# Full 128-row, 128-column weights for the products of a triangular inversion, and a new order of the front's pieces, in a two-layer encoder on one core

## The chip, the core and the metric

The kernel runs on one core of one Trainium2 chip. The metric is device microseconds of one launch, the median of several launches. The engines named here are TensorE (PE, with PEld for its loads of weights), VectorE (DVE), ScalarE (ACT), GpSimd (POOL) and SyncE (SP), which issues the DMAs.

## What is computed

Two encoder layers over 512 tokens of width 1024. Each layer has a differential attention branch, a gated delta rule in both directions (four heads, chunks of 64 tokens), gates that merge the two, and an MLP. The change touches the triangular solve in the delta rule, and the order of the work ahead of it:

```python
L = jnp.where(strict, jnp.einsum('bhncd,bhnmd->bhncm', kb, k) * decay, 0.0)
T = lax.linalg.triangular_solve(eye + L, jnp.broadcast_to(eye, L.shape), left_side=True,
                                lower=True, unit_diagonal=True)
u = jnp.einsum('bhncm,bhnme->bhnce', T, v * beta[..., None])
```

## The kernel before, in words

The kernel treats the 512 tokens as four tiles (NT) of 128. It first records every operation with its operands. A planner (`Plan.schedule`) then lists the recorded operations onto five in-order queues (PE, ACT, DVE, POOL, SP). It uses the costs of the function `cost`, priorities, and the free buffers of each pool. What a queue holds is fixed when the program is built, and at run time each engine waits at its own head. So a plan that puts an instruction too early makes that engine wait, with everything behind it. All operations carry one line of the kernel file, L431, where they are issued, so tiles are told apart by name.

In each layer a "front" comes after the first norm. It is a list of pieces in the string `ORDER[l]`: `d` (three projections of one delta-rule head, with a convolution on DVE), `z` (its gate's projection), `q`, `k`, `v` (projections for two attention heads), `a` (chunk matrices of a delta-rule head), `b` (inversion of the 32x32 diagonal blocks of two heads, a chain of small DVE operations on the tile XA), `c` (the rest of a head's delta rule) and `t` (one attention head). The recording order is only the planner's priority. The engines' real order follows from the plan.

Names that the steps need: `d_dn`, `d_z`, `d_da` and `d_g` are PSUM tiles of the dense projections. Their products take weights and activations in a split form (`whi`, `wlo` and `hh`, `hl`), and `wlo_...` is made on DVE. `kqv` is a projection after its convolution (`cacc`) and activation. `tokT` is its transpose on PE. `qkT`, `rot` and `dt` belong to attention's q and k. `zg` is the gate of `z`.

The products of the inversion stand in `gdn_c`, once for each layer, head and direction d. `pn` multiplies L by the inverse of its diagonal blocks, giving `NTr`. Then three products `px` (n = 1, 2, 3) extend X by one band of 32 columns (NB) each. Each of these is a group of four matmuls in float32, one for each token tile; the trace holds two records for each float32 matmul. With two layers, four heads, two directions and four products there are 64 groups. The call `four(name, lhsT, rhs, rows, cs)` has `lhsT` as weights and `rhs` as the moving operand. In the kernel before, the weights are only the rows that are needed:

```python
rows, cs = (slice(0, m), slice(NB * n, P)) if d == 0 else (slice(0 if n == 1 else P - m, P), slice(0, m))
ps, op = four("px", NTr[ks, :, rows], X[ks, d, :, cs], rows, cs)
```

with m = 96, 64, 32. So the weights are 96 (d = 0) or 128 (d = 1) columns wide for n = 1, 64 for n = 2 and 32 for n = 3, and the moving operand has 96, 64 and 32 columns. For `pn` the weights have 128 columns (d = 0) or 96 (d = 1), and the moving operand 96.

Of the kernel before, what the change touches and what calls it, by code (L numbers as in the profile page):

```python
# [17 lines left out]
P = 128  # L18
# [12 lines left out]
NB = 32  # L31
# [153 lines left out]
class Plan:  # L185
# [13 lines left out]
    def add(self, engs, fn, args, kw):  # L199
# [37 lines left out]
        op.shared = fn != "memset" and not any(v.t.cls == "B" for v in ins + outs)  # L237
        op.tried = set()
        op.cost = [cost(e, fn, dst, ins, kw) for e in engs]
        self.ops.append(op)  # L240
        return op
# [209 lines left out]
def cost(eng, fn, dst, ins, kw):  # L451
    n = int(np.prod(dst.shape[1:]))
    ptr = sum(isinstance(kw.get(k), View) for k in ("scalar", "scalar1", "scale", "bias"))
    psum = any(v.t.cls == "B" for v in ins)
    if ins:
        n = max([n] + [int(np.prod(v.shape[1:])) for v in ins]) if eng != "pe" else n
    if eng == "sp":
        return int(np.prod(dst.shape)) * 4 / 360.0
    if eng == "pe":
        if fn == "transpose":  # L460
            return 109.0
        if kw["lhsT"].dt == F32:
            return 4 * max(n, 32) / 2.4 + 9.0
        return 120.0 if n <= 256 else n / 2.4 + 14.0
    if eng == "act":
        return (51.0 if psum else 93.0) + 93.0 * ptr + n / 1.2 + (93.0 if kw.get("accum_out") is not None else 0.0)
    if eng == "dve":
        if fn == "memset":
            return 8.0 + n / 0.96
        if fn == "reciprocal":  # L470
            return 69.0 + 6.25 * n
        return 69.0 + 60.0 * ptr + n / 0.96
    if fn == "memset":
        return 36.0 + n / 1.2
    return 150.0 + (1.66 if any(v.a.strides[-1] == 0 for v in ins) else 2.1) * n
# [11 lines left out]
GS, NYF, KEEPM = (3, 5), 2, (3, 2)  # L487


ORDER = ("d0 a0 d1 a1 z1 z0 q0 b0 z2 c0 c1 d3 d2 a3 k0 a2 b2 c2 z3 q1 k1 v1 v0 t0 t2 t3 c3 t1",  # L490
         "d0 k1 d1 q0 d2 z1 a0 z0 d3 k0 z2 a1 b0 c0 a2 v0 t0 c1 a3 b2 q1 c2 z3 v1 c3 t3 t1 t2")


@with_exitstack
def encoder(ctx, tc, a, out):
# [3 lines left out]
    pe, act, dve, pool, sp = (Eng(pl, e) for e in ("pe", "act", "dve", "pool", "sp"))  # L499
    ad, dp = Eng(pl, "act", "dve"), Eng(pl, "dve", "pool")  # L500
# [10 lines left out]
    def Y(shape, name, dt=F32, **kw):  # L511
        return pl.tile("Y", shape, name, dt, **kw)

    def F(shape, name, dt=F32, **kw):
        return pl.tile("F", shape, name, dt, **kw)
# [4 lines left out]
    def B(shape, name, **kw):  # L520
        return pl.tile("B", shape, name, **kw)
# [105 lines left out]
    for i in range(2):  # L627
        half = slice(512 * i, 512 * i + 512)
        ps = B([P, 512], "cps")
# [143 lines left out]
    for l in range(DEPTH):  # L773
# [9 lines left out]
        for w in range(2):  # L783
            pool.tensor_tensor(out=cg[:, w], in0=ccos, in1=bc(gain[:, l, w], 1, NT), op=ALU.mult, after=[normed])
            pool.tensor_tensor(out=sg[:, w, :, 0:32], in0=csin[:, :, 0:32], in1=bc(gain[:, l, w, 32:64], 1, NT), op=ALU.mult,
                               after=[normed])
            pool.tensor_tensor(out=sg[:, w, :, 32:64], in0=csin[:, :, 32:64], in1=bc(gain[:, l, w, 0:32], 1, NT), op=ALU.mult,
                               after=[normed])
# [271 lines left out]
        def gdn_c(h, XA):  # L1060
            k_, ktok, vtok = (kqv[(i, h)] for i in (1, 3, 4))
            L, PT, qd, s2, sv, sk, qal = (st_[h][n] for n in ("L", "PT", "qd", "s2", "sv", "sk", "qal"))

            X = F([P, 2, NT, P], "X")
            DT = F([P, 2, NT, P], "DT")
# [11 lines left out]
            def four(name, lhsT, rhs, rows, cs):  # L1077
                ps = B([P, NT, P], name)
                for t in range(NT):
                    op = pe.matmul(ps[rows, t, cs], lhsT=lhsT[:, t], rhs=rhs[:, t], start=True, stop=True)  # L1080
                return ps[rows, :, cs], op

            for d in range(2):
                NTr = Y([P, NT, P], "NT")
                if d == 0:
                    c1, full, ks = slice(0, P - NB), slice(0, P), slice(0, P)
                else:
                    c1, full, ks = slice(NB, P), slice(0, P - NB), slice(0, P - NB)  # L1090
                    pool.memset(NTr[ks, :, 0:NB], 0.0, after=[gate["inv"]])
                ps, gate["pq"] = four("pn", L[:, d, :, full], DT[:, d, :, c1], full, c1)
                ad.copy(NTr[full, :, c1], ps)
                for n in range(1, 4):
                    m = P - NB * n
                    rows, cs = (slice(0, m), slice(NB * n, P)) if d == 0 else (slice(0 if n == 1 else P - m, P), slice(0, m))
                    ps, op = four("px", NTr[ks, :, rows], X[ks, d, :, cs], rows, cs)
                    x = X[rows, d, :, cs]
                    if n == 1:
                        dve.tensor_tensor(out=x, in0=ps, in1=x, op=ALU.add)  # L1100
                    else:
                        ad.copy(x, ps)

            Ss, V2, S2 = [None], [Y([P, 2, 2, P], "V") for i in range(2)], [Y([P, 2, 2, P], "S") for i in range(2)]
            for s in range(NT):
# [10 lines left out]
                for d in range(2):  # L1116
                    full = pe.matmul(pv[:, d], lhsT=X[:, d, tt[d]], rhs=R[:, d] if s else vtok[:, tt[d]], start=True, stop=True)
                if s < NT - 1:
                    Vk = Y([P, 2, P], "Vk")
                    for d in range(2):  # L1120
                        full = dve.tensor_scalar(out=Vk[:, d], in0=pv[:, d], scalar1=sk[:, d, tt[d]:tt[d] + 1], scalar2=None,
                                          op0=ALU.mult, after=[full])
                for d in range(2):
                    act.activation(V2[s // 2][:, s % 2, d], pv[:, d], AF.Copy, scale=sv[:, d, tt[d]:tt[d] + 1],
                                   after=[full])
# [41 lines left out]
        gate = {}  # L1167
# [82 lines left out]
        XA = {}  # L1250
        for piece in ORDER[l].split():
            kind, h = piece[0], int(piece[1])
            hp = h & 2
            if hp not in XA:
                XA[hp] = F([P, NB, NB], "XA")
            if kind == "d":
                dn_proj(h)
            elif kind == "a":
                gdn_a(h, XA[hp])
            elif kind == "b":  # L1260
                gdn_b(h, 2, XA[hp])
            elif kind == "z":
                z_proj(h)
            elif kind == "c":
                gdn_c(h, XA[hp])
            elif kind in "qk":
                da_qk("qk".index(kind), h)
            elif kind == "v":
                da_v(h)
            else:  # L1270
                attention(h)
# [42 lines left out]
        for q in range(4):  # L1314
# [88 lines left out]
            def pair(name):  # L1403
                return [B([P, 512], name, grp="m2", keep=KEEPB) for b in range(2)]

            chain = {}
            X, Z_, Yq = pair("m2x"), pair("m2z"), pair("m2y")
# [151 lines left out]
```

## Time and profile before

| what | value |
|---|---|
| median of 3 runs | 1633.89 us (1632.93 to 1635.31) |
| the profiled execution | 1633.24 us |
| its span, first to last instruction | 1631.5 us |
| PE busy | 1593.6 us, 98% of the span |
| DVE busy | 1347.1 us, 83% |
| ACT busy | 832.0 us, 51% |
| POOL busy | 167.5 us, 10% |
| granted clock of PE, mean | 0.992 |

The profile is of one execution, 0.65 us under the median of the runs. Times on the timeline count from the first instruction. A record's duration includes the part in which the next one already runs, so what a record costs PE is read from one start to the next start. The front of layer 0 lies at about 20 to 245 us, and that of layer 1 at about 840 to 1050 us. The products lie in four clusters, at about 173 to 192, 286 to 305, 989 to 1008 and 1105 to 1122 us.

### The profile page before, as it was taken

The page shows a single profiled execution, that of the slowest core. Times are in us where ns is not written, and L with a number is a line of the kernel's source. Part 1 is how long each engine was busy: PE and PEld are TensorE (multiplying, and loading weights), DVE is VectorE, ACT ScalarE, POOL GpSimd, SP SyncE. Part 2 cuts the span into 40 slices and gives each one's busy share as a digit, 9 for nine tenths or more (in the row PEclk, how much of TensorE's full clock was granted, in tenths as well). Part 3 has the DMA queues.
Part 4 walks back from the last instruction along what each step waited for, and adds up shares of the span by engine and source line. Part 5 has one row for each costly group of instructions (what it writes and reads, how often), then busy time and mean ns, then how long its engine had stood idle before and what let it go on. Part 6 is the DMA issues. An engine that isn't in the chain of part 4 may idle for free.

```text
span 1631.5 us, 25364 instructions
## 1 busy us (share of the span) xinstructions
PE 1593.6 (98%) x9136; PEld 1384.2 (85%) x9136; DVE 1347.1 (83%) x2999; ACT 832.0 (51%) x1592; POOL 167.5 (10%) x170
## 2 busy tenths in 40 slices
PE   6997999999999999999989999999999999999998
PEld 4787998888899888888879889988889988888887
DVE  7998798799799989998889986986947885767676
ACT  4553353566256645454666434735733674636361
POOL 0240250001300000000014210400003000000000
PEclk9998999999999999999999999999999999999999
DMA  9332435634668484939232405245233525252542
GB/s 380 118 110 78 130 84 172 192 97 156 258 219 311 155 322 156 347 136 335 103 138 85 141 34 160 65 140 116 91 143 126 210 78 206 79 205 80 204 156 78
DMA packets 107728, 260.78 MB, mean 160 GB/s; under 512 B 27841, under 2 KB 40769, under 8 KB 107602
## 3 DMA queue, kind: packets, MB, share of 16 engines
q1 hardware_dynamic: 107602, 259.16, 46.5%
q8 instruction: 72, 1.18, 0.3%
q14 instruction: 54, 0.44, 0.1%
HBM read 242.31 MB, written 16.81 MB: 159 GB/s over the span
## 4 chain that ended last, share of the span: by engine, by line
PE 91%; DVE 7%; issue 1%; ACT 1%; DMA 0%; SPq 0%; POOL 0%; DVEq 0%; POOLq 0%; ACTq 0%
PE d_m L431 18%; PE d_g L431 11%; PE m2x L431 11%; PE d_dn L431 7%; PE d_da L431 7%; PE d_out L431 6%; PE m2y L431 5%; PE d_m1f L431 3%; PE d_brb L431 3%; PE d_bra L431 3%; PE m2z L431 3%; PE d_z L431 2%; PE px L431 2%; PE sc L431 2%; PE po L431 2%; PE pv L431 2%
## 5 line engine op out<-in xcount | busy, mean ns | idle before, releaser
L431 PE MATMUL d_m<-hh,whi_m 128*128 128x512 f32 x448 | 174.5, 389 | 0.0
L431 PE MATMUL d_m<-hl,whi_m 128*128 128x512 f32 x448 | 174.5, 389 | 0.0
L431 PE MATMUL d_m<-hh,wlo_m 128*128 128x512 f32 x448 | 174.4, 389 | 0.0
L431 DVE TENSOR_TENSOR m2lo<-m,m2hi 128x1024 fp32r<-128x1024 f32 x112 | 132.6, 1220 | 9.8 <-ACT m2hi L431 8.4
L431 ACT CAST m2hi<-m 128x1024 fp32r<-128x1024 f32 x112 | 114.1, 1050 | 50.4 <-DMA m<-in_w_m_dram 22.7
L431 DVE SCALAR_TENSOR_TENSOR ada<-ada,cb 128x1024 f32<-128x1024 f32 x96 | 118.2, 1242 | 7.3 <-DMA ada<-in_ada_w_dram 7.2
L431 PE MATMUL d_da<-wlo_da,hh 128*128 128x256 f32 x384 | 110.4, 290 | 2.0 <-DVE wlo_da L431 2.0
L431 PE MATMUL d_da<-whi_da,hl 128*128 128x256 f32 x384 | 111.6, 291 | 0.0
L431 PE MATMUL d_da<-whi_da,hh 128*128 128x256 f32 x384 | 111.2, 290 | 0.0
L431 ACT ACTIVATE relu<-d_m 128x512 f32<-128x512 f32 x56 | 33.5, 599 | 138.2 <-PE d_m L431 138.1
L431 PE MATMUL d_g<-hh,wlo_g 128*128 128x512 f32 x256 | 102.4, 400 | 0.0
L431 PE MATMUL d_g<-hh,whi_g 128*128 128x512 f32 x256 | 102.3, 400 | 0.0
L431 PE MATMUL d_g<-hl,whi_g 128*128 128x512 f32 x256 | 101.4, 397 | 0.0
L431 PEld LDWEIGHTS d_m<-hh,whi_m 128*128 128x128 f32 x448 | 84.1, 188 | 17.5
L431 PEld LDWEIGHTS d_m<-hh,wlo_m 128*128 128x128 f32 x448 | 84.1, 188 | 17.4
L431 PEld LDWEIGHTS d_m<-hl,whi_m 128*128 128x128 f32 x448 | 84.1, 188 | 17.3
L431 ACT CAST whi_m<-raw_m 128x1024 fp32r<-128x1024 f32 x56 | 58.8, 1050 | 52.3 <-DMA raw_m<-in_w_mlp_dram 39.3
L431 PE MATMUL d_dn<-hh,wlo_dn 128*128 128x512 f32 (+1 forms) x208 | 80.0, 388 | 2.9 <-DVE wlo_dn L431 2.9
L431 PE MATMUL d_dn<-hl,whi_dn 128*128 128x512 f32 (+1 forms) x208 | 79.8, 384 | 0.0
L431 DVE TENSOR_TENSOR m<-m,m 128x1024 f32<-128x1024 f32 x64 | 77.6, 1220 | 0.0
L431 PE MATMUL d_dn<-hh,whi_dn 128*128 128x512 f32 (+1 forms) x208 | 77.2, 382 | 0.0
L431 DVE TENSOR_TENSOR wlo_m<-raw_m,whi_m 128x1024 fp32r<-128x1024 f32 x56 | 68.0, 1222 | 10.4 <-ACT whi_m L431 9.7
(324 smaller groups left out, 4760.9 us busy)
## 6 DMA issues: line engine op xcount, KB each, us to landing
m<-in_w_m_dram SPq DMA_DIRECT2D x112, 512.0 KB, 4.5
ada<-in_ada_w_dram SPq DMA_DIRECT2D x96, 512.0 KB, 6.5
raw_m<-in_w_mlp_dram SPq DMA_DIRECT2D x56, 512.0 KB, 5.2
raw_g<-in_w_g_dram SPq DMA_DIRECT2D x32, 512.0 KB, 4.8
raw_out<-in_w_out_dram SPq DMA_DIRECT2D x32, 512.0 KB, 4.1
raw_dn<-in_w_dn_dram SPq DMA_DIRECT2D x24, 512.0 KB, 5.4
raw_da<-in_w_da_dram SPq DMA_DIRECT2D x24, 512.0 KB, 4.3
xs<-xT SPq DMA_DIRECT2D x24, 256.0 KB, 3.5
```

The costliest lines, as they stand in the source:

```text
L431: op.ins = getattr(eng[op.eng[0]], fn)(*[real(v) for v in op.args], **{k: real(v) for k, v in op.kw.items()})
```

## The change

All 64 groups of products now load the whole 128x128 matrix as weights and write all 128 partitions of the PSUM tile. Only the rows and columns used before are read from it afterwards. The number of matmuls and their moving columns (96, 64, 32) stay. For direction 0 a small POOL memset of 32 columns of `NTr` is added, eight in all. The planner's cost of a float32 matmul gets another floor, and both `ORDER` strings are new.

```diff
         if kw["lhsT"].dt == F32:
-            return 4 * max(n, 32) / 2.4 + 9.0
+            return max(4 * n / 2.4 + 9.0, 111.0 * dst.shape[0] / P)
...
-ORDER = ("d0 a0 d1 a1 z1 z0 q0 b0 z2 c0 c1 d3 d2 a3 k0 a2 b2 c2 z3 q1 k1 v1 v0 t0 t2 t3 c3 t1",
-         "d0 k1 d1 q0 d2 z1 a0 z0 d3 k0 z2 a1 b0 c0 a2 v0 t0 c1 a3 b2 q1 c2 z3 v1 c3 t3 t1 t2")
+ORDER = ("d1 d0 a0 a1 z1 z0 z2 q0 b0 c0 c1 d3 d2 a3 a2 b2 c2 k1 z3 k0 v1 c3 q1 t2 v0 t3 t1 t0",
+         "d0 k1 d1 d2 z1 a0 d3 z2 v0 q0 k0 a1 z0 b0 c0 a2 c1 t0 a3 b2 c2 z3 v1 q1 c3 t3 t1 t2")
...
-                    op = pe.matmul(ps[rows, t, cs], lhsT=lhsT[:, t], rhs=rhs[:, t], start=True, stop=True)
+                    op = pe.matmul(ps[:, t, cs], lhsT=lhsT[:, t], rhs=rhs[:, t], start=True, stop=True)
...
-                if d == 0:
-                    c1, full, ks = slice(0, P - NB), slice(0, P), slice(0, P)
-                else:
-                    c1, full, ks = slice(NB, P), slice(0, P - NB), slice(0, P - NB)
-                    pool.memset(NTr[ks, :, 0:NB], 0.0, after=[gate["inv"]])
-                ps, gate["pq"] = four("pn", L[:, d, :, full], DT[:, d, :, c1], full, c1)
-                ad.copy(NTr[full, :, c1], ps)
+                c1, c0 = (slice(0, P - NB), slice(P - NB, P)) if d == 0 else (slice(NB, P), slice(0, NB))
+                pool.memset(NTr[:, :, c0], 0.0, after=[gate["inv"]])
+                ps, gate["pq"] = four("pn", L[:, d], DT[:, d, :, c1], slice(0, P), c1)
+                ad.copy(NTr[:, :, c1], ps)
...
-                    ps, op = four("px", NTr[ks, :, rows], X[ks, d, :, cs], rows, cs)
+                    ps, op = four("px", NTr, X[:, d, :, cs], rows, cs)
```

The plan moves instructions on every engine. Three places follow. A row reads operation, written tile, operands, shape.

PE in layer 0, where the second `z` block ends (about 85 us in the trace of before), in the kernel before:

```order
L431 MATMUL d_z<-hh_437,wlo_z_774 128x512
L431 MATMUL d_z<-hh_485,whi_z_532 128x512
L431 MATMUL d_z<-hl_493,whi_z_532 128x512
L431 MATMUL d_z<-hh_485,wlo_z_774 128x512
L431 MATMUL d_da<-whi_da_552,hh_185 128x256
L431 MATMUL d_da<-whi_da_552,hl_190 128x256
L431 MATMUL d_da<-wlo_da_827,hh_185 128x256
```

and PE at the same place now:

```order
L431 MATMUL d_z<-hh_437,wlo_z_773 128x512
L431 MATMUL d_z<-hh_485,whi_z_532 128x512
L431 MATMUL d_z<-hl_493,whi_z_532 128x512
L431 MATMUL d_z<-hh_485,wlo_z_773 128x512
L431 MATMUL d_z<-hh_185,whi_z_552 128x512
L431 MATMUL d_z<-hl_190,whi_z_552 128x512
L431 MATMUL d_z<-hh_185,wlo_z_826 128x512
```

A third `z` block of 24 matmuls now stands ahead of the attention projections here; before, it stood some 250 rows later.

ACT in layer 0, at the projections of the last two delta-rule heads (about 112 to 133 us), in the kernel before:

```order
L431 CAST whi_da_1348<-raw_da_1265 128x1024
L431 ACTIVATE cacc<-d_dn_1217,cols 128x512
L431 CAST whi_da_1392<-raw_da_1284 128x1024
L431 ACTIVATE cacc<-d_dn_1353,cols 128x512
L431 ACTIVATE kqv_1402<-cacc 128x512
L431 ACTIVATE kqv_1417<-cacc 128x512
L431 COPY tok_1430<-tokT 128x512
L431 ACTIVATE kqv_1441<-cacc 128x512
```

and ACT there now:

```order
L431 ACTIVATE cacc<-d_dn_1328,cols 128x512
L431 ACTIVATE kqv_1393<-cacc 128x512
L431 COPY tok_1417<-tokT 128x512
L431 CAST whi_da_1422<-raw_da_1278 128x1024
L431 ACTIVATE sqj,gss_1427<-tok_1417 128x128 x4
L431 ACTIVATE cacc<-d_dn_1381,cols 128x512
L431 ACTIVATE kqv_1443<-cacc 128x512
L431 ACTIVATE kqv_1457<-cacc 128x512
L431 COPY tok_1470<-tokT 128x512
L431 ACTIVATE kqv_1495<-cacc 128x512
```

In both, the `cacc` of the next head's first projection stands ahead of two `kqv`; now a third `kqv`, with its copy and its squares, stands in the same stretch as well.

DVE in layer 1, at the end of the first XA chain (about 978 to 984 us), in the kernel before:

```order
L431 TENSOR_TENSOR XA<-XA,btmp 64x30
L431 SCALAR_TENSOR_TENSOR rqu<-rqr 128x8
L431 MEMSET XA 64x32
L431 TENSOR_TENSOR rqu<-rqu,rqv 128x8
L431 TENSOR_TENSOR wlo_da_10702<-raw_da_10241,whi_da_10444 128x1024
L431 SCALAR_TENSOR_TENSOR rqr<-rqu,rqr 128x8
L431 TENSOR_TENSOR wlo_da_10709<-raw_da_10284,whi_da_10527 128x1024
L431 SCALAR_TENSOR_TENSOR rqu<-rqr 128x8
L431 TENSOR_TENSOR wlo_da_10719<-raw_da_10393,whi_da_10574 128x1024
L431 TENSOR_TENSOR rqu<-rqu,rqv 128x8
L431 TENSOR_TENSOR wlo_da_10729<-raw_da_10490,whi_da_10648 128x1024
```

and DVE there now:

```order
L431 TENSOR_TENSOR XA<-XA,btmp 64x30
L431 SCALAR_TENSOR_TENSOR dars<-rqu,rqr 128x8
L431 MEMSET XA 64x32
L431 TENSOR_SCALAR qsc<-dars 128x2x2x2
L431 TENSOR_REDUCE dass<-dsq 128x8
L431 TENSOR_TENSOR dt_10627<-d_da,sgn 128x8x32
L431 TENSOR_SCALAR rqv<-dass 128x8
L431 TENSOR_TENSOR wlo_da_10635<-raw_da_10271,whi_da_10487 128x1024
L431 TENSOR_TENSOR dt_10627<-d_da,sgn 128x8x32
```

Four halves of attention weights (`wlo_da`) stood behind the chain. Now one does, and the matmuls that use it stand behind `pn` on PE.

## Rows read from the trace of the kernel before

**Rows 1.** Page, part 1 (busy us, share) and part 4 (chain that ended last)

```profile
PE 1593.6 (98%) x9136; PEld 1384.2 (85%) x9136; DVE 1347.1 (83%) x2999; ACT 832.0 (51%) x1592; POOL 167.5 (10%) x170
...
PE 91%; DVE 7%; issue 1%; ACT 1%; DMA 0%; SPq 0%; POOL 0%; DVEq 0%; POOLq 0%; ACTq 0%
```

**Rows 2.** Timeline, PE, layer 1: start, duration, operation, tiles, weights rows*columns, moving, records

```profile
989.31 0.28 PE L431 MATMUL d_da<-whi_da,hl 128*128 128x256 f32 x1
989.43 1.04 PE L431 MATMUL pn<-DT,L 128*128 128x96 f32 x8
...
990.45 0.28 PE L431 MATMUL d_da<-whi_da,hh 128*128 128x256 f32 x1
...
991.04 0.28 PE L431 MATMUL d_da<-wlo_da,hh 128*128 128x256 f32 x1
991.16 0.84 PE L431 MATMUL px<-X,NT 128*96 128x96 f32 x8
...
991.99 0.28 PE L431 MATMUL d_da<-whi_da,hl 128*128 128x256 f32 x1
...
992.70 0.28 PE L431 MATMUL d_da<-whi_da,hl 128*128 128x256 f32 x1
992.91 0.68 PE L431 MATMUL px<-X,NT 128*64 128x64 f32 x8
...
993.74 0.28 PE L431 MATMUL d_da<-whi_da,hh 128*128 128x256 f32 x1
```

**Rows 3.** Timeline, PE, layer 1, a group with 32 columns

```profile
1001.90 0.28 PE L431 MATMUL d_da<-whi_da,hl 128*128 128x256 f32 x1
1002.12 0.44 PE L431 MATMUL px<-X,NT 128*32 128x32 f32 x8
...
1002.71 0.36 PE L431 MATMUL px<-X,NT 96*128 96x96 f32 x2
```

**Rows 4.** Timeline, PE, MLP of layer 0: one moving column, full weights

```profile
497.42 0.28 PE L431 MATMUL d_m1f<-hh,wlo_m1f 128*128 128x256 f32 x1
497.54 0.51 PE L431 MATMUL nss<-ones,nsq 128*128 128x1 f32 x4
...
498.10 0.28 PE L431 MATMUL d_m1f<-hl,whi_m1f 128*128 128x256 f32 x1
```

**Rows 5.** Windows: length, busy PE, PEld, DVE, ACT, POOL, granted clock, DMA

```profile
123.00:130.00 7.00, 1.08 (x6) 0.65 (x5) 5.89 (x13) 1.70 (x3) 0.00 (x0) 0.80 0.42 150
130.00:137.00 7.00, 4.67 (x17) 3.89 (x16) 7.00 (x13) 1.75 (x3) 1.07 (x3) 0.50 0.00 0
976.00:990.00 14.00, 11.83 (x86) 11.39 (x85) 10.16 (x28) 3.19 (x5) 2.09 (x2) 0.88 0.60 197
```

**Rows 6.** Timeline, PE, layer 0; in brackets idle time before it, and releaser

```profile
123.12 0.39 PE L431 MATMUL d_dn<-hh,whi_dn 128*128 128x512 f32 x1
123.35 0.39 PE L431 MATMUL d_dn<-hl,whi_dn 128*128 128x512 f32 x1
129.66 1.09 PE L431 MATMUL tokT<-cst,kqv 128*128 128x128 f32 x4 [5.92 <-DVE kqv L431]
...
133.93 0.80 PE L431 MATMUL d_dn<-hh,wlo_dn 128*128 128x512 f32 x1 [2.33 <-DVE wlo_dn L431]
```

**Rows 7.** Timeline, ACT, layer 0

```profile
122.87 0.69 ACT L431 ACTIVATE cacc<-d_dn,cols 128x512 f32<-128x512 f32 x1 [3.75 <-PE d_dn L431]
```

**Rows 8.** Timeline, DVE, layer 0

```profile
124.11 0.69 DVE L431 SCALAR_TENSOR_TENSOR kqv<-kqv,cacc 128x512 f32<-128x512 f32 x1 [2.96 <-ACT kqv L431]
124.72 0.36 DVE L431 TENSOR_TENSOR XA<-XA,btmp 64x210 f32<-64x210 f32 x1
```

**Rows 9.** Groups by form, DVE, 100 to 140 us: busy us, mean ns, idle before

```profile
L431 DVE TENSOR_TENSOR wlo_dn<-raw_dn,whi_dn 128x1024 fp32r<-128x1024 f32 x5 | 6.1, 1211 | 0.0
...
L431 DVE TENSOR_TENSOR rot<-d_da,cg 128x512 f32<-128x512 f32 x1 | 0.7, 677 | 0.0
```

**Rows 10.** Timeline, PE, layer 1, ahead of the products

```profile
980.31 0.45 PE L431 MATMUL d_da<-wlo_da,hh 128*128 128x256 f32 x1 [2.00 <-DVE wlo_da L431]
```

## The prediction

> **What bounds the kernel now.** I read the page first, then the timeline around the products, then the stretches in which PE does not run. The page shows PE busy for 98% of the span and 91% of the chain that ended last on PE [rows 1]. PE's share would say little if its records overlapped waits, so the reader should look at starts: in the four clusters of products a dense matmul follows a product and a product a dense matmul without a gap. What a product costs PE is therefore paid at the end of the kernel, unless PE later waits for something that a longer product lets finish in time. The only long waits of PE in the fronts' second halves are two: in layer 0 at 123 to 137 us, where PE idles 5.92 and 2.33 us and then runs at a granted clock of 0.50 (the lower level, 1.2 GHz) [rows 5, 6], and in layer 1 at 978 to 984 us, 2.00 us of idle time with a mean clock of 0.88 over 976 to 990 us [rows 5, 10]. The change works on two things: the price of 64 groups of products, and these waits.
>
> **The price of a group of four products.** I take an isolated group between dense matmuls and measure from the start of the last dense record before it to the start of the second dense record after it, less two dense records. A dense record of 256 columns takes 0.12 us (989.31 to 989.43). In [rows 2]: weights of 128 columns, 96 moving: 990.45 - 989.31 - 0.24 = 0.90 us. Weights of 96 columns, 96 moving: 991.99 - 991.04 - 0.24 = 0.71. Weights of 64 columns, 64 moving: 993.74 - 992.70 - 0.24 = 0.80. In [rows 3], weights and moving of 32 columns: 1002.71 - 1001.90 - 0.24 = 0.57. The first two have the same moving operand and differ by 0.19 us in eight records, so the width of the weights sets the price, not the moving stream. The third is dearer than its eight starts suggest: the start ahead of it is 0.21 us after the dense record, not 0.12, and the way out is long too. A group with 64 or 32 columns pays for entering and leaving.
>
> In one (layer, head), both directions, there are eight groups: `pn` 0.90 and 0.71; n = 1 0.71 and 0.90 (the last one has 96 rows but 128 columns, priced as the first); n = 2 twice 0.80; n = 3 twice 0.57. That is 5.96 us, times eight 47.7 us.
>
> Afterwards all eight have 128 columns. For 96 moving columns the price is the measured 0.90. For 64 and 32 moving columns with full weights the trace has no row; I bound it with the case of one moving column: [rows 4] gives 498.10 - 497.42 - 0.24 = 0.44 us for two matmuls, 0.88 for four. So a full load costs 0.88 to 0.90 whether 1 or 96 columns move, and 64 and 32 lie between. At 0.90 the eight are 7.2 us, times eight 57.6: **9.9 us more**; at 0.88 for the four narrow ones 56.3 in all if even the wide ones fell to it, 8.6 more. I take 10, near the upper end, since [rows 2] is the same product in the same stretch. Half falls in each layer. It lies on the path, because PE runs without a gap in the clusters. What would hide it is a wait of PE behind the products; in the clusters I see none above a microsecond.
>
> The same can be split: wider loads cost, and the entering and leaving of 32 narrow groups is saved. On the saved part: the start ahead of the 64-column group is 0.09 us late [rows 2]. The Trainium skill, TensorEngine Tiling (Array Packing), Key Properties, says that changing the tiling mode drains the engine, which speaks for this change; here it is about 0.09 us on the way in and like that on the way out, some 6 us over 32 groups, already inside the four prices. Against the change speaks the Trainium skill, TensorE: Matmul & The Clock Gate, section on LDWEIGHTS: a load takes the number of its columns over 1.2 ns, however many rows it has. By that page a record with 128 instead of 32 columns would take 107 instead of 27 ns, an estimate of 0.64 us more for a group of n = 3 without the saved switches, against the 0.33 that the rows give with them.
>
> **The other edits of the products.** The new memset of 32 columns on POOL, eight times, hangs on a gate that is long past when `pn` comes, on an engine busy for 10% [rows 1]: nothing. The copies out of PSUM keep their columns (the copy of `NTr` for d = 1 has 128 partitions now, not 96, with the same columns): nothing.
>
> **The order, layer 0.** PE idles at `tokT`, which transposes the third projection of a head [rows 6]. Its input is released by DVE. DVE is full there (7.00 of 7.00 us at 130 to 137 [rows 5]), and ACT adds a wait: its `cacc` of the next projection waits for PE at the head of the queue (3.75 us of idle time [rows 7]) with a `kqv` behind it, for which DVE then waits 2.96 us [rows 8]. The order now puts 24 `d_z` matmuls ahead; at 0.23 us each (123.12 to 123.35 [rows 6]) that is 5.5 us of PE's work done before the wait. By itself it would take away nearly all of it. But DVE's queue between the same two landmarks (the third `kqv` of the second head in the list and the third `kqv` of the next) has grown too, from 74 instructions to 84: one more `wlo` (1.21 us [rows 9]), one more `rot` (0.68 [rows 9]), two halves of `dt`, about another `rot`, and six more XA steps (0.36 each [rows 8]), 4.7 us in sum. And ACT still has the same `cacc` ahead of the same two `kqv`, with a copy, a cast and four squares ahead of it. So the gain in PE's work and the delay in DVE's nearly cancel: I take **0**, from -4 (ACT's wait is gone and half of the low clock) to +5 (ACT's wait is paid twice, the clock stays low longer).
>
> **The order, layer 1.** PE's wait was for a `wlo_da` that stood on DVE behind the XA chain, which itself stood behind a `zg` [rows 10]. Now one `wlo_da` stands there, and PE needs it only behind `pn`; ahead of `pn` PE has a whole `z` block of 24 matmuls (5.5 us). The idle time and the lower clock are worth 14.00 - 11.83 = 2.2 and 0.12 x 14 = 1.7 us, together 3.9 [rows 5]. In exchange three heads' projections now follow each other without attention blocks between, so a `tokT` can wait for DVE there: 72 records of 0.23 us are 16.5 us of PE's time per head against twelve convolutions, three `wlo` and three `kqv` on DVE, next to the chunk matrices of the head before. I take **-2**, from -4 to +3. What PE would be late for next is the second half of the front, which is dense with `d_da` and `d_g`.
>
> **The sum.** 1633.24 us (the profiled execution) + 10 + 0 - 2 = 1641.2. The runs' median lies 0.65 us above the profiled execution; I put 1641.5. Low end: +8.6 - 4 - 4 gives 1633.8; high end: +10 + 5 + 3 is 1651.9 with both orders at their worst, which I cut to 1648.
>
> **The rivals.** (1) The moving stream sets the price, as the planner's new cost has it, and the loads hide under the running matmul. Then a group costs 0.71 for 96 columns and, in proportion to the columns and without switches, 0.48 for 64 and 0.25 for 32: 4.3 us for eight, 34.4 in all, 13.3 less than before, and with the order **1619**. It decides at one point: whether eight starts of a group with 32 moving columns and full weights take 0.25 or 0.9 us. Against it stand both halves of [rows 2] and the one moving column of [rows 4]. The Trainium skill's page on TensorE gives such a gap in its section on the back-to-back gap: moving columns over 2.4 ns plus 2.5, with no term for the load. (2) The order takes it back: the layer 0 wait is worth 5.92 + 2.33 us of idle time and about half of the 4.67 us at the low clock, 10.6 in all [rows 5, 6], with layer 1's 3.9 together 14.5. If all of it went, 1633.9 + 10 - 14.5 = 1629.4, faster; if some 9 went, **1635**, no difference that can be told. For it speaks the `z` block ahead, against it DVE's 4.7 us. (3) The waits grow: ACT's head of queue delays two `kqv`, PE idles for 8 us at `tokT` and for 3 more in layer 1, each with a stretch at the lower clock: **1647**. That the narrow weights are still loaded is ruled out: the built program's products write 128 partitions.
>
> **How the numbers follow.** About 0.2% (3.3 us) is what a measurement can tell from no change. The forecast, 1641.5, gets 0.62 (0.57 of it slower, 0.05 within 0.2%); rival 1 0.07, faster; rival 2 0.17 (0.12 within, 0.05 faster); rival 3 0.14, slower. So slower 0.71, same 0.17, faster 0.12. The range 1634 to 1648 holds the forecast's bounds, the nearer half of rival 2 and most of rival 3.
>
> **What the profile after would show.** Right: isolated groups of `px` with 64 and 32 moving columns at 0.88 to 0.90 us, no late start ahead of them, and the four clusters about 10 us longer in sum. Also right: a wait of several us at a `tokT` near 130 us with the clock at 0.50, and none of 2 us ahead of layer 1's first `pn`. Wrong: groups of n = 3 below 0.6 us (rival 1), PE without idle time at 120 to 140 us (rival 2), or a new wait at a place that I haven't named, above all in the attention part, whose order also changes and which I have left at nothing.

## The result

| what | before | after |
|---|---|---|
| median of 4 runs | 1633.68 us (1632.93 to 1635.31) | 1643.28 us (1640.32 to 1644.90) |
| the profiled execution | 1633.24 us | 1644.00 us |
| its span | 1631.5 us | 1641.9 us |

The ratio is 1.0055, with a 95% interval of 1.0038 to 1.0073. The change makes the kernel 9.6 us slower. The forecast was 1641.5 us in a range of 1634 to 1648, with 0.71 for slower. The total came out 1.8 us above the forecast; two of the three terms in the sum were off by more than that, in opposite directions.

### The profile page after: what moved, and what is told of

It is laid out like the page before. It is cut to its first block, busy times and chain, and to the rows that moved or that the text cites. A ratio compares the mean times of both kernels' runs of the same rounds, so it can differ in the third digit from the quotient of the medians.

```text
span 1641.9 us, 25362 instructions
## 1 busy us (share of the span) xinstructions
PE 1604.3 (98%) x9136; PEld 1399.6 (85%) x9136; DVE 1348.3 (82%) x2993; ACT 835.1 (51%) x1598; POOL 165.0 (10%) x178
## 4 chain that ended last, share of the span: by engine, by line
PE 92%; DVE 6%; ACT 1%; issue 1%; DMA 0%; SPq 0%; DVEq 0%; ACTq 0%
PE d_m L431 18%; PE d_g L431 11%; PE m2x L431 11%; PE d_dn L431 7%; PE d_da L431 7%; PE d_out L431 6%; PE m2y L431 5%; PE d_m1f L431 3%; PE d_brb L431 3%; PE m2z L431 3%; PE d_bra L431 3%; PE px L431 3%; PE d_z L431 2%; PE sc L431 2%; PE po L431 2%; PE pv L431 2%
## 5 line engine op out<-in xcount | busy, mean ns | idle before, releaser
L431 DVE SCALAR_TENSOR_TENSOR cacc<-d_dn,cols,cacc 128x510 f32<-128x510 f32 (+1 forms) x96 | 70.9, 741 | 5.5 <-ACT cacc L431 5.3
```

What stands on the lines that cost most here:

```text
L431: op.ins = getattr(eng[op.eng[0]], fn)(*[real(v) for v in op.args], **{k: real(v) for k, v in op.kw.items()})
```

## The profile after

Of the page, part 1 (busy time and share) and the share of the last chain by engine; they answer to [rows 1]:

```profile
PE 1604.3 (98%) x9136; PEld 1399.6 (85%) x9136; DVE 1348.3 (82%) x2993; ACT 835.1 (51%) x1598; POOL 165.0 (10%) x178
...
PE 92%; DVE 6%; ACT 1%; issue 1%; DMA 0%; SPq 0%; DVEq 0%; ACTq 0%
```

PE is the bound as before, with as many records and 10.7 us more of busy time.

The timeline of PE in layer 1, isolated groups of products (start, duration, weights rows*columns, moving, records); they answer to [rows 2] and [rows 3]:

```profile
993.49 0.28 PE L431 MATMUL d_da<-whi_da,hh 128*128 128x256 f32 x1
993.61 1.03 PE L431 MATMUL px<-X,NT 128*128 128x96 f32 x8
...
994.62 0.28 PE L431 MATMUL d_da<-wlo_da,hh 128*128 128x256 f32 x1
...
1010.28 0.28 PE L431 MATMUL d_da<-whi_da,hl 128*128 128x256 f32 x1
1010.40 0.98 PE L431 MATMUL px<-X,NT 128*128 128x32 f32 x8
...
1011.41 0.27 PE L431 MATMUL d_da<-whi_da,hh 128*128 128x256 f32 x1
```

Read as in the prediction: 994.62 - 993.49 - 0.24 = 0.89 us with 96 moving columns and 1011.41 - 1010.28 - 0.24 = 0.89 with 32. A third of the moving columns costs the same. The group with 32 starts 0.12 us after the dense record, so the late start is gone.

For all products of a cluster I take the time from the start of the last dense record before its first product to the end of the second record after its last one (the start of the record behind it), and take off every other matmul at its own pitch (0.227 us for a dense record of 512 columns, 0.120 for one of 256, 0.112 for a product of the chunks, 0.089 for a transpose):

| cluster | before, us | after, us |
|---|---|---|
| layer 0, first | 18.81 - 6.92 = 11.89 | 20.68 - 6.36 = 14.32 |
| layer 0, second | 19.66 - 7.92 = 11.74 | 21.21 - 6.79 = 14.42 |
| layer 1, first | 19.24 - 7.54 = 11.71 | 20.32 - 5.96 = 14.36 |
| layer 1, second | 17.77 - 5.65 = 12.11 | 19.56 - 5.20 = 14.36 |
| sum | 47.45 | 57.46 |

That is 10.0 us more. The rest is the order. The first `d_out` of layer 0 (the projection of the branches' output, behind the front) starts 9.07 us later than before (448.07 and 457.14). Of these, 5.11 are products (28.74 - 23.63), so layer 0's order costs 3.96. Up to the first `d_da` of layer 1 another 0.66 us come on top, in the norm. From there to PE's last transposes (`yT`, 1626.32 and 1636.84) only 0.80 us more are lost, of which the products would be 4.90 (28.72 - 23.82); layer 1's order gives back 4.1.

Where layer 0 waits (PE, with the idle time in brackets), as [rows 6]:

```profile
128.78 0.40 PE L431 MATMUL d_dn<-hl,whi_dn 128*128 128x512 f32 x1
137.07 1.09 PE L431 MATMUL tokT<-cst,kqv 128*128 128x128 f32 x4 [7.89 <-DVE kqv L431]
...
141.35 0.80 PE L431 MATMUL d_dn<-hh,wlo_dn 128*128 128x512 f32 x1 [2.34 <-DVE wlo_dn L431]
```

Windows, after (length, busy PE, PEld, DVE, ACT, POOL, granted clock, DMA share): one from the `tokT` near 102 us to the one at 137.07, one in the wait, and layer 1 ahead of its first products, as [rows 5]:

```profile
102.01:137.07 35.06, 26.75 (x131) 21.89 (x131) 30.47 (x85) 13.25 (x25) 7.77 (x15) 0.96 0.28 88
...
134.00:141.00 7.00, 1.94 (x8) 1.68 (x8) 7.00 (x15) 1.85 (x3) 0.00 (x0) 0.50 0.00 0
978.00:992.00 14.00, 14.00 (x98) 12.97 (x97) 11.34 (x52) 4.22 (x6) 3.88 (x3) 1.00 0.52 140
```

The first window, in the kernel before, between the same two landmarks:

```profile
102.35:129.66 27.31, 20.77 (x95) 16.64 (x96) 24.32 (x75) 11.11 (x22) 4.39 (x6) 0.95 0.43 144
```

DVE and then ACT between the same landmarks, after; they answer to [rows 8] and [rows 7]:

```profile
123.64 0.69 DVE L431 SCALAR_TENSOR_TENSOR kqv<-kqv,cacc 128x512 f32<-128x512 f32 x1 [0.22 <-ACT kqv L431]
...
131.43 0.69 DVE L431 SCALAR_TENSOR_TENSOR kqv<-kqv,cacc 128x512 f32<-128x512 f32 x1 [2.95 <-ACT kqv L431]
...
136.25 0.67 DVE L431 SCALAR_TENSOR_TENSOR kqv<-kqv,cacc 128x512 f32<-128x512 f32 x1
```

```profile
127.59 0.59 ACT L431 COPY tok<-tokT 128x512 f32<-128x512 f32 x1 [3.99 <-PE tokT L431]
...
130.78 0.62 ACT L431 ACTIVATE kqv<-cacc 128x512 f32<-128x512 f32 x1
```

The first of these `kqv` is the one that ACT holds behind a `cacc` that waits for PE, as in [rows 7, 8]. It comes 21.63 us after the first landmark (123.64 - 102.01), and before it came after 21.76 (124.11 - 102.35). The growth lies behind it: from there to PE's `tokT` it is 13.43 us (137.07 - 123.64), and before it was 5.55 (129.66 - 124.11). DVE has the convolution of one more projection there, with its chain steps and its `kqv` (131.43 to 136.25, 4.8 us), and a new wait of 2.95 us for ACT, whose copy at the head of the queue waits 3.99 us for a `tokT` on PE.

The stretch at the lower clock, after and then before:

```profile
133.92:147.57 13.65, 8.16 (x25) 6.65 (x26) 13.58 (x26) 3.71 (x12) 0.00 (x0) 0.50 0.30 98
```

```profile
127.16:137.40 10.24, 5.41 (x18) 4.58 (x19) 10.24 (x19) 2.74 (x7) 1.20 (x3) 0.50 0.00 0
```

Layer 1 has neither idle time nor a lower clock left (14.00 of 14.00 us, clock 1.00). In layer 0 PE idles for 2 us more than before, and the granted clock is 0.50 (the lower level, 1.2 GHz) in the second half of the wait and behind it.

## Experiments: products or order

In all kernels below but the one with another price, the queues hold the plan of the kernel before or after instruction for instruction, except where a move is named.

**Full weights, plan of before.** Each product is planned as the narrow one and issued as the full one (the last two arguments); the small memset stands right ahead of the copy that fills the rest of `NTr`.

```diff
-ps, op = four("px", NTr[ks, :, rows], X[ks, d, :, cs], rows, cs)
+ps, op, _ = four("px", NTr[ks, :, rows], X[ks, d, :, cs], rows, cs, NTr, X[:, d, :, cs])
```

> The plan of the kernel before is kept, instruction by instruction on every queue; only the products' weights become 128x128 (with the eight small memsets they need). Theory: the wider loads are paid whole at the end, 57.5 us of products instead of 47.5, so 10.0 us over the kernel before: ratio 1.0061, about 1643.7 us, with the stalls of before unchanged (5.92 us at a tokT of layer 0, 2.00 us at a wlo_da of layer 1). Rival: the old order has waits behind the products that hide a part, or the plan falls out of step; then 1637 to 1640, or 1647 and more, with a stall in the four clusters that was not there.

Measured: 1643.99 us (5 runs; before on the same chip 1633.86), ratio 1.0066, interval 1.0052 to 1.0079. The waits of layer 0 are those of before:

```profile
128.68 1.09 PE L431 MATMUL tokT<-cst,kqv 128*128 128x128 f32 x4 [5.92 <-DVE kqv L431]
...
132.95 0.80 PE L431 MATMUL d_dn<-hh,wlo_dn 128*128 128x512 f32 x1 [2.33 <-DVE wlo_dn L431]
```

The wider loads alone cost the whole loss, as expected, and nothing hides them.

**Narrow weights, plan of after.** The reverse; again the last two arguments are issued.

```diff
-ps, op = four("px", NTr, X[:, d, :, cs], rows, cs)
+ps, op = four("px", NTr, X[:, d, :, cs], rows, cs, NTr[ks, :, rows], X[ks, d, :, cs])
```

> The plan of the changed kernel is kept on every queue; only the products go back to their narrow weights. Theory: the order gives +4.0 us in layer 0 (longer wait at tokT and more time at the lower clock) and -4.1 us in layer 1, together 0: ratio 0.9995 to 1.0005, about 1633.7 us, products 47.5 us. Rival: the order itself is what costs the 9 to 10 us, and the products are hidden; then 1640 or more.

Measured: 1633.52 us (11 runs), ratio 0.9999, interval 0.9990 to 1.0008. The clusters sum to 47.0 us, and PE's waits in layer 0 are those of after:

```profile
136.30 1.09 PE L431 MATMUL tokT<-cst,kqv 128*128 128x128 f32 x4 [7.88 <-DVE kqv L431]
...
140.58 0.80 PE L431 MATMUL d_dn<-hh,wlo_dn 128*128 128x512 f32 x1 [2.34 <-DVE wlo_dn L431]
```

So the new order is worth nothing in sum, as +4.0 and -4.1 say; the two layers' orders have no run each of their own.

**Other widths.** What sets a group's price when weights and moving operand differ? By direction and n, the columns of weights and the moving columns that are issued in the plan of before:

```diff
+WIDE = {(0, 2): (slice(0, 96), None), (0, 3): (slice(0, 64), None),
+        (1, 2): (None, slice(0, 96)), (1, 3): (None, slice(0, 96))}
```

> The plan of the kernel before; the products have other widths: d = 0, n = 2 has 96 columns of weights and 64 moving (before 64 and 64); d = 0, n = 3 has 64 of weights and 32 moving (before 32 and 32); d = 1, n = 2 has 64 of weights and 96 moving; d = 1, n = 3 has 32 of weights and 96 moving. Theory: the columns of the weights alone set a group's price, with a surcharge at 64 and 32: 0.71, 0.80, 0.80 and 0.57 us; sum about 1.1 us over the kernel before. Rival: the wider of weights and moving operand sets it: the last two rise to 0.9 us each, and 3.6 to 4 us come on top. Rival: the moving stream alone sets it: the first stays at 0.80, the second at 0.57.

Measured: one run, 1639.07 us, and clusters of 53.4 us in sum, 5.9 more than before, where the expectation had 1.1 and the first rival some 5. The groups, in the order of the expectation: 0.70, 0.78, 1.00, and the last one below. First 96 columns of weights with 64 moving, then 32 of weights with 96 moving between dense records of 512 columns:

```profile
995.60 0.28 PE L431 MATMUL d_da<-whi_da,hl 128*128 128x256 f32 x1
995.72 0.81 PE L431 MATMUL px<-X,NT 128*96 128x64 f32 x8
...
996.54 0.28 PE L431 MATMUL d_da<-whi_da,hh 128*128 128x256 f32 x1
...
1126.47 0.48 PE L431 MATMUL d_g<-hh,wlo_g 128*128 128x512 f32 x1
1126.88 0.85 PE L431 MATMUL px<-X,NT 96*32 96x96 f32 x8
...
1128.00 0.39 PE L431 MATMUL d_g<-hl,whi_g 128*128 128x512 f32 x1
```

The last group in the kernel before, with 32 moving columns:

```profile
1121.09 0.48 PE L431 MATMUL d_g<-hh,wlo_g 128*128 128x512 f32 x1
1121.50 0.44 PE L431 MATMUL px<-X,NT 96*32 96x32 f32 x8
...
1122.20 0.39 PE L431 MATMUL d_g<-hl,whi_g 128*128 128x512 f32 x1
```

From the dense record to the second one after: 1.53 us against 1.11, with the same weights. My expectation, that the columns of the weights alone set the price, is wrong. In all the widths that ran, the wider of the two sets it: within a group the starts are 31 to 32 ns apart with 32 and 32 columns, 58 with 64 of weights and 32 or 64 moving, 82 to 83 with 96 moving and 32 or 64 of weights, 84 to 85 with 96 of weights and 64 or 96 moving, and 111 to 112 with 128 of weights. The first and second group follow the weights, the third and fourth the moving operand. In the change the weights are always the wider one, so its price hangs on them.

**The planner's price.** The planner holds a product for half of what it takes.

```diff
-            return max(4 * n / 2.4 + 9.0, 111.0 * dst.shape[0] / P)
+            return max(4 * n / 2.4 + 9.0, 222.0 * dst.shape[0] / P)
```

> The changed kernel, but the planner's floor for a float32 matmul is 222 ns instead of 111 (two records of 111 ns, as the trace has it); the order moves in many places. Theory: the products are paid at the end whatever the planner believes, 57.5 us; the time stays at that of the changed kernel, 1643, within 3 us either way by where the waits of layer 0 fall. Rival: the planner's wrong price has put work in bad places, and the true one gives back some of the 10 us: 1638 us or less.

Measured: 1640.68 us (4 runs), ratio 1.0040, interval 1.0027 to 1.0054. The clusters cost 57.9 us, as in the changed kernel (57.5). That is within the 3 us of the expectation, and the rival asked for 1638 or less, which it isn't. It is 2.6 us under the changed kernel, in another series of runs and with an order that differs in many places. Its profiled execution has waits of 7.33 and 2.34 us in layer 0 and 10.2 us at the clock 0.50 there instead of 13.7; what in the order brings this is not shown.

## Experiments: the waits of layer 0

All five have the narrow products and the plan of after, so they stand against 1633.5 us. Each moves a few instructions on one or two queues.

**ACT first.** DVE waits for a `kqv` that stands on ACT behind other work:

```diff
 order = pl.schedule()
+order = moved(order, (1422, 1523, 1980, 1616, 1617, 1618, 1619), 1455)
```

The numbers are operations as recorded: a copy of `tokT`, a `cacc`, a cast and four squares go behind the `kqv` that is 1455.

> The kernel with narrow products and the changed kernel's plan, and one move on ACT's queue in layer 0: the kqv that DVE waits 2.95 us for (131.43 us in the changed kernel's trace) goes ahead of a copy, a cacc, a cast and four squares. Theory: DVE's wait falls from 2.95 to about 0.5 us, and PE's wait at the next tokT by as much, from 7.9 to 5.5 us: 2.4 us less than the kernel with narrow products and this plan, about 1631.3 us, a little more if the clock returns earlier. Rival: DVE's own backlog sets the tokT, and the moved kqv only lets DVE wait later (for the next projection of PE): the wait of PE stays at 7.5 to 7.9 us, 1633.7 us.

Measured: 1630.95 us (10 runs), ratio to before 0.9986, interval 0.9977 to 0.9995; 2.6 us less than without the move.

```profile
139.14 1.09 PE L431 MATMUL tokT<-cst,kqv 128*128 128x128 f32 x4 [4.84 <-DVE kqv L431]
...
143.42 0.80 PE L431 MATMUL d_dn<-hh,wlo_dn 128*128 128x512 f32 x1 [2.34 <-DVE wlo_dn L431]
```

DVE's wait of 2.97 us at that `kqv` is gone and PE's falls by 3.0 us: what DVE waited for ACT was passed on to PE whole. The expectation had 5.5 us for the wait and 1631.3 for the time.

**The chain later.** Ten steps of the chain on XA go behind the third `kqv` of the stretch (1490) on DVE, on top of ACT first.

```diff
+order = moved(order, (1067, 1068, 1069, 1070, 1071, 1072, 1073, 1074, 1075, 1076), 1490)
```

> The kernel e3_act_first (narrow products, the changed kernel's plan, kqv ahead on ACT), and one move on DVE's queue in layer 0: ten steps of the chain on XA that stand between the convolutions go behind the third kqv. Theory: DVE is full there, so the third kqv comes earlier by the ten steps, some 0.3 us each from start to start, 3.0 us; PE's wait at tokT falls from 4.84 to about 1.9 us and the time by 3, to about 1628 us. Rival: the chain on XA is late then; its blocks go through memory and PE waits as long at the first pn near 176 us: 1631 us, with a new wait there. Rival: the third kqv waits for something other than DVE's queue: the wait stays at 4.8 us.

Measured: 1634.07 us (10 runs), ratio 1.0006, interval 0.9996 to 1.0015. That is none of the three. PE's waits, and DVE between them:

```profile
133.88 1.09 PE L431 MATMUL tokT<-cst,kqv 128*128 128x128 f32 x4 [3.29 <-DVE kqv L431]
...
141.82 0.80 PE L431 MATMUL d_dn<-hh,wlo_dn 128*128 128x512 f32 x1 [6.00 <-DVE wlo_dn L431]
```

```profile
136.21 0.40 DVE L431 TENSOR_TENSOR btmp<-XA 64x240 f32<-64x240 f32 x1
136.64 0.40 DVE L431 TENSOR_TENSOR XA<-XA,btmp 64x240 f32<-64x240 f32 x1
137.07 0.40 DVE L431 TENSOR_TENSOR btmp<-XA 64x240 f32<-64x240 f32 x1
...
137.83 1.52 DVE L431 SCALAR_TENSOR_TENSOR cacc<-d_dn,cols,cacc 128x511 f32<-128x511 f32 x2
139.27 0.39 DVE L431 TENSOR_TENSOR btmp<-XA 64x238 f32<-64x238 f32 x1
```

And in the kernel with ACT first, where a step stands between two parts of a convolution:

```profile
134.42 0.74 DVE L431 SCALAR_TENSOR_TENSOR cacc<-d_dn,cols,cacc 128x511 f32<-128x511 f32 x1
135.08 0.39 DVE L431 TENSOR_TENSOR btmp<-XA 64x238 f32<-64x238 f32 x1
135.39 0.73 DVE L431 SCALAR_TENSOR_TENSOR cacc<-d_dn,cols,cacc 128x511 f32<-128x511 f32 x1
```

The wait at `tokT` fell (4.84 to 3.29) but the steps then stood ahead of `wlo_dn`, for which PE waited 6.00 us instead of 2.34: the sum rose from 7.18 to 9.29. The chain is one dependent step after another. By itself a step takes 0.43 us from start to start (136.21, 136.64, 137.07) and a convolution's part 0.72 (two in a row from 137.83 to 139.27); one step and one part in turn take 0.97 for both (134.42 to 135.39), not 1.15. By these rows ten steps torn from their partners cost about 1.8 us of DVE's time, an estimate.

**Four moves.** On top of that, `wlo_dn` (1537) goes ahead of the first `kqv` on DVE, and on ACT that `kqv` (1416) ahead of the `cacc` (1484) that waits for PE.

```diff
+order = moved(order, (1537,), 1064)
+order = moved(order, (1484,), 1416)
```

> The kernel e5_chain_later with two more moves in the same stretch of layer 0: wlo_dn, whose inputs are there from about 116 us, goes on DVE from behind the third kqv to ahead of the first one, where DVE waited 1.65 us for ACT; and on ACT that first kqv goes ahead of a cacc that waits 3.75 us for PE. Theory: PE's wait of 2.34 us for wlo_dn goes, the two moves cancel on DVE, and with shorter waits the clock is at its lower level for less or not at all, 1 to 3 us: together 3 to 5 us under e5_chain_later, about 1624 us. Rival: PE only comes earlier to the next wait (the next tokT or the first pn): 1627 to 1628 us.

Measured: 1633.24 us (11 runs), ratio 0.9997, interval 0.9988 to 1.0006. The wait for `wlo_dn` is gone, and PE waits for the next `kqv` instead, the place that the rival named. But the time is neither the 1624 us expected nor the rival's 1627 to 1628: the sum of the waits is 9.4 us where it was 9.3, so the moves gave back nothing clear of the spread.

```profile
135.83 0.63 PE L431 MATMUL tokT<-cst,kqv 128*128 128x128 f32 x4 [3.30 <-DVE kqv L431]
...
143.77 1.11 PE L431 MATMUL tokT<-cst,kqv 128*128 128x128 f32 x4 [6.14 <-DVE kqv L431]
```

**The same without moving the chain.**

```diff
-order = moved(order, (1067, 1068, 1069, 1070, 1071, 1072, 1073, 1074, 1075, 1076), 1490)
```

> The kernel e3_act_first with wlo_dn ahead of the first kqv on DVE and this kqv ahead of the cacc on ACT; the chain on XA stays where the changed kernel's plan has it. Theory: by the same sum DVE loses only the 1.65 us that it waited for ACT, less what wlo_dn takes there: PE's waits in the stretch fall from 7.2 to about 5.8 us, 1629.5 us. Rival: the moves only exchange one wait for another: 7.2 us, 1631 us.

Measured: 1628.93 us (5 runs), ratio 0.9968, interval 0.9956 to 0.9981. The waits are 6.0 us in sum; time and waits are as expected.

```profile
137.78 0.63 PE L431 MATMUL tokT<-cst,kqv 128*128 128x128 f32 x4 [4.23 <-DVE kqv L431]
...
142.05 1.11 PE L431 MATMUL tokT<-cst,kqv 128*128 128x128 f32 x4 [1.73 <-DVE kqv L431]
```

**The chain behind all of it.** Against the kernel with four moves, fourteen steps go behind the last `kqv` of the stretch and the `wlo_dn` after it (1571).

```diff
-order = moved(order, (1067, 1068, 1069, 1070, 1071, 1072, 1073, 1074, 1075, 1076), 1490)
+order = moved(order, tuple(range(1067, 1081)), 1571)
```

> The kernel e7_four_moves, but the steps of the chain on XA go further back on DVE: fourteen steps behind the second kqv after the stretch and the wlo_dn that follows it, so that no wait of PE in the stretch has them ahead of it. Theory: DVE's work up to PE's last tokT of the stretch sets the sum of PE's waits there (9.4 us in e7_four_moves, wherever they lie), and thirteen steps less are some 4 us less: waits of 5.4 us in sum, 1629 us, and the waits fall one for one with DVE's work. Rival: the chain's end is late by as much, and PE waits 3 to 4 us at the first pn: 1633 us, as e7_four_moves.

Measured: 1627.86 us (5 runs), ratio 0.9963, interval 0.9950 to 0.9977.

```profile
134.48 0.63 PE L431 MATMUL tokT<-cst,kqv 128*128 128x128 f32 x4 [3.30 <-DVE kqv L431]
...
138.06 1.12 PE L431 MATMUL tokT<-cst,kqv 128*128 128x128 f32 x4 [0.98 <-DVE kqv L431]
...
161.81 0.66 PE L431 MATMUL tokT<-cst,kqv 128*128 128x128 f32 x4 [1.40 <-DVE kqv L431]
```

There is no wait at the first `pn`, so the rival falls, and time and waits are near the expected 1629 and 5.4 us. The waits of the stretch (115 to 145 us), the time at the lower clock that begins there, and PE's way from the last `tokT` ahead of the waits (126 to 132 us) to the first `pn`, all of the profiled execution, beside the medians of the runs:

| kernel | PE's waits, us | sum | at the clock 0.50 | PE to the first `pn` | median |
|---|---|---|---|---|---|
| plan of after | 7.88 + 2.34 | 10.2 | 13.7 us | 49.45 us | 1633.5 |
| ACT first | 4.84 + 2.34 | 7.2 | 10.2 | 46.73 | 1631.0 |
| chain later | 3.29 + 6.00 | 9.3 | 13.7 | 48.89 | 1634.1 |
| four moves | 3.30 + 6.14 | 9.4 | 6.8 | 47.50 | 1633.2 |
| without moving the chain | 4.23 + 1.73 | 6.0 | 6.8 | 44.47 | 1628.9 |
| chain behind all | 3.30 + 0.98, 1.40 later | 5.7 | 6.8 | 44.74 | 1627.9 |

Within one execution PE's way to the first `pn`, on which it runs the same 254 records in each kernel, follows the sum of the waits within about 1.2 us, wherever the waits lie, and the medians follow it within about 1.5 us. The profiled executions as a whole do not: the one of the plan of after took 1631.26 us and the one with ACT first 1634.61, the slowest of its ten runs. They differ ahead of the stretch, above all by PE's wait at a `tokT` near 101 to 105 us (1.33 and 3.85 us; see the last section), which the table leaves out. What counts in the stretch is what shortens DVE's way to the last `tokT`: ACT's delay taken out, a `wlo_dn` put where DVE waits anyway, or work put behind it. The last two kernels, with narrow weights, are 4.9 and 6.0 us under the kernel before. The last stands 1.1 us under the one ahead of it, within the runs' spread, so whether moving the chain adds to the other moves is open.

## Why the prediction was right, and where its steps were not

- **The price of the products: right.** I took 10 us from 57.6 - 47.7; the clusters give 57.5 - 47.5, and the kernel with full weights alone is 10.1 us over before. The bound by the one moving column [rows 4] was good: 32 moving columns cost 0.89. Its wording, that the width of the weights sets the price and not the moving stream, was too wide, as the widths show: it holds where the weights are the wider one. The estimate from the Trainium skill, TensorE: Matmul & The Clock Gate, section on LDWEIGHTS, was 0.64 us more for a group of n = 3 without the saved switches. The starts in the group went from 31 to 32 ns to 111 to 112, which is 0.64 for eight; with the switches the group rose by 0.32, from 0.57 to 0.89. For the difference rule and trace agree; each start is 4 to 5 ns above the rule's 27 and 107.
- **Rival 1 (the moving stream): fell** at the point it named, 0.89 us instead of 0.25. A gap that counts the moving columns alone doesn't fit starts of 111 to 112 ns with 32 moving columns.
- **Layer 0's order: the term was mis-sized**, 0 where 4.0 was measured, inside its bounds of -4 to +5. PE's side was right: 5.5 us more work ahead of the wait, measured 26.75 - 20.77 = 6.0. DVE's side was not: I had 4.7, and the two windows give 35.06 - 27.31 = 7.75 (6.15 busy, 1.6 idle). The step that failed is that I added up DVE's extra instructions over the whole window, as if DVE ran through it without a stop, and called two sums of equal size a cancellation. In both kernels DVE waits for ACT, and so for PE, at the `kqv` behind the held `cacc` (2.96 and 0.22 us), 21.8 and 21.6 us after the first landmark, and what DVE does ahead of it cost nothing here. What counts is its way from there to the `tokT`: 5.55 us before, 13.43 now, of which 4.8 are one more convolution and 2.95 a wait for ACT that I had left to the upper bound. The wait has its experiment (ACT first, 3.0 us of it came to PE); the convolution is read from the rows alone. Of the 4.0 us, 2.0 are idle time of PE; PE also runs 8.16 us of its work at the lower clock instead of 5.41, and half of the difference, 1.4 us, is lost there, an estimate. The rest, some 0.6 us, has no cause shown.
- **Layer 1's order: right in kind, too small**, -2 where -4.1 was measured, at the lower bound that I gave. All of the idle time and the low clock went, 3.9 by [rows 5, 10], and the new `tokT` wait that I set against it did not come. No run has layer 1's order alone; the figure stands on the landmarks and on the sum of nothing for both orders.
- **Rivals 2 and 3**: half of each was there, the return in layer 1 and the longer wait in layer 0, and they cancelled. That ACT's head of queue delays a `kqv` is shown by the kernel with ACT first.
- **What I left at nothing** held, but for 0.66 us in the norm between the layers, which has no experiment.
- **The total** came near partly by luck: the two errors of the order, +4.0 and -2.1, left 1.9 us. The low end of the sum, 1633.8, was counted from the profiled execution and the high end from the median; from the median the low end is 1634.5.

## What to carry to other kernels

Price a small float32 matmul by the wider of its weights' columns and its moving columns, and by a measured start-to-start time in the same stretch; widening the weights to save the late start of a narrow group (0.09 us on the way in here) only pays if that costs more than the added columns. When you compare the work ahead of a wait, find the last point at which that engine itself waited for another, and count from there: work ahead of it costs nothing as long as the engine still waits there. Where PE waits several times in one stretch for one full engine, add up the waits: a move on that engine that only changes which wait comes first changes nothing, and a dependent chain pulled from between other work makes that engine slower.

## What the runs showed of the hardware that I had not expected

A small operation of DVE can take eight times as long beside POOL. In the kernel with ACT first, the timeline of DVE and then that of POOL:

```profile
85.48 0.16 DVE L431 SCALAR_TENSOR_TENSOR rqr<-rqu,rqr 128x8 f32<-128x8 f32 x1
85.67 1.29 DVE L431 SCALAR_TENSOR_TENSOR rqu<-rqr 128x8 f32<-128x8 f32 x1
87.00 1.22 DVE L431 TENSOR_TENSOR rqu<-rqu,rqv 128x8 f32<-128x8 f32 x1
```

```profile
85.65 1.29 POOL L431 TENSOR_TENSOR w<-w,cst 128x512 f32<-128x512 f32 x1 [8.37 <-DVE rqr L431]
86.90 1.29 POOL L431 TENSOR_TENSOR qd<-kqv,gb 128x512 f32<-128x512 f32 x1
```

Operations of 128x8 take 0.16 us alone and 1.2 to 1.3 here, each ending with POOL's operation. A larger one is held up too: in the changed kernel a `wlo_dn` at 107.68 us took 2.33 us in place of 1.21 beside a POOL operation (107.60 to 108.92); it lies ahead of the `kqv` that ACT holds, so PE lost nothing by it. Around 85 us eight of POOL's operations stand in a row, and how many small ones of DVE fall among them differs between executions with the same order up to there. Seven of the profiled executions have that order. In them, the time that DVE's operations at 78 to 103 us take beyond the usual length of the same operation and shape (its lower quartile in the trace) is 4.7, 4.8, 5.9, 6.9, 8.0, 8.0 and 8.1 us, and PE's wait at the `tokT` near 101 to 105 us is 1.33, 1.44, 2.46, 2.67, 3.73, 3.75 and 3.85 us. I take this for a part of the spread of some 6 us among the runs of these kernels; no run tests it. The Trainium skill, GPSIMD Engine Reference, section Specifications, says that POOL's way to SBUF is shared with VectorE and that they contend where the VectorE instruction has two inputs in SBUF or runs in a two-port mode. The rows shown, of operations with two inputs, agree with it.
